# A two-layer trunk on one core: the order of the mixer's conv products, value products and scores, the place of the conv taps, and the splitting of the output weights

## The chip, the cores and the metric

The kernel runs on one NeuronCore of a Trainium2 chip. The core has five engines with an instruction queue each: PE (TensorE, matrix products), DVE (VectorE), ACT (ScalarE), POOL (GpSimd) and SP (SyncE, which here only starts transfers). POOL starts transfers too. An engine works through its queue in order; an instruction that waits for another engine, or for a transfer, holds up all that stands behind it on its own engine.

The metric is device time of one execution in microseconds (us), the median over several executions.

## The reference

The program computes a trunk of two layers on 512 tokens with 1024 features, in fp32. Each layer is a half-step feed-forward block, a mixer, another half-step feed-forward block and a norm. The change lies in the mixer alone:

```python
n = rms_norm(h, mix_norm[l]);  p = n @ w_in[l]
u_conv, q, k, v, q_mem = jnp.split(p, splits, axis=-1)
a, gate = jnp.split(u_conv, 2, axis=-1)              # 384 channels each
y = a * jax.nn.sigmoid(gate)
y = causal_depthwise_conv(y, w_dw, 31 taps) + b_dw
y_conv = jax.nn.silu(layer_norm(y, g, b))
y_swa = sliding_window_attention(rope(norm(q)), rope(norm(k)), v, sinks)  # 6 heads of 64, window 128
y_mem = memory_attention(norm(q_mem), mk, mv)                             # 4 heads, 256 memory rows
h = h + jnp.concatenate([y_conv, y_swa, y_mem], axis=-1) @ w_out[l]
h = h + 0.5 * swiglu(rms_norm(h, ffn2_norm[l]), ffn2_w1[l], ffn2_w3[l], ffn2_w2[l])
```

## The kernel before

**Layout.** Activations are held transposed: 128 partitions carry features of one of 8 chunks, 512 tokens lie along the free axis. Every product is made of three fp32r matmuls on a high and a low part of each operand (`mm3`, L172 to L176: hi·hi, then the two cross products). So each weight tile is loaded as a raw fp32 tile by SP (3 raw buffers, tag "raw") and split in two. `weights(..., V)` does it by an ACT copy (L143, the high part) and a DVE subtract (L144, the low part). `weights(..., G)` does it by two ACT copies (L148 the high part, L149 the negative of the raw tile) and a transfer that POOL starts and that adds the weights from memory to that negative (L150, about 0.9 us on POOL per start). The raw tile is free again when the last reader has read it: the DVE subtract in the first way, the second ACT copy in the other.

**Who sets the order.** A list of steps in the string `ORDER` is walked once per layer, and a scheduler that estimates durations decides how the work of these steps is interleaved on each engine; `tc.issue_after(x)` makes it place an instruction behind `x`. `queued()` places PE work behind the last matmul issued. The result is one fixed list per engine.

**The mixer's steps.** `c<c><i>`: half i of conv chunk c (24 matmuls of 128x512; half 1 holds the gate: a sigmoid on ACT, L669, then the gated input goes to `ypad`). `q`, `Q`: query products and their transposition to columns. `v`, `V`: value products (24 matmuls of 128x384) and their transposition. `a`: attention in ten groups of two (or one) 128-row blocks. For each group there are scores on PE, their row maxima on DVE (L751 and L752 for memory groups, L765 to L767 for window groups), Exp on ACT (L777), transposes on PE (L783) copied by ACT (L785), products with the values on PE (L794), division on DVE, and for a finished block transposes to the output operand (PE L817, ACT L143 `ghi`, DVE L144 `glo`). `t<c>`: the 31 taps of a conv chunk, one DVE instruction of 128x512 each (L871 the first, L874 the other 30), 93 per layer. `s`: the conv branch's layer norm and Silu: two sums over the three chunks on POOL (L880, L881), a matmul with ones that gives the mean (L883), three DVE subtracts of it (L886), squares on ACT (L234) added on DVE (L246), sums by matmul (L200), the root on POOL (L191), a spreading matmul (L213), the multiply (L891), Silu (L892) and a split.

**After the steps** stands the output product. For each of 8 output chunks there are 5 products with the attention's chunks (120 matmuls of 128x512 in all, weight tiles of 128x640, four split in each of the two ways) and then 3 with the conv chunks (72 matmuls, weight tiles of 128x768 named `ours`, one for two output chunks, split by ACT and DVE). The attention products need no result of the conv branch, so they are the work that PE has while the conv branch's norm is made. The next feed-forward block's weight tiles (128x1024, `in_w1b`, `in_w3b`) follow in the same raw buffers.

Of the kernel before, what the change touches and what calls it, by code (L numbers as in the profile page):

```python
# [18 lines left out]
P = 128  # L19
# [27 lines left out]
ORDER = "c00 c01 q0 c10 q1 c11 Q0 q2 v0 Q1 q3 v1 Q2 v2 v3 Q3 V0 V1 c20 V2 V3 a t0 t1 t2 s"  # L47
# [14 lines left out]
def trunk(ctx: ExitStack, tc: tile.TileContext, xT, memT, pos, w1a, w3a, w2a, w1b, w3b, w2b,  # L62
# [19 lines left out]
    def mm():  # L82

        turn[0] += 1
        return bank([P, S], "mm" if turn[0] % 4 else "cf")
# [526 lines left out]
    def mixer(l, x, st, last):  # L612
# [31 lines left out]

        def conv_half(c, i):
            nonlocal R
            ps = bank([P, S], "po") if c == 2 else mm()
            with queued():
                project(ps, weights(wconv[l, c, i], 1024, V if c + i < 2 else G, spare() if c == 2 else None), x)
            if c == 0:  # L650
                with queued():
                    if i == 0:
                        V.tensor_copy(rc, rms_cols(st, D))
                    else:
                        R = kept(spread(rc), "R", V)
            halves.append((c, i, ps))
            while halves and R is not None:
                gate(*halves.pop(0))
# [72 lines left out]
        def scored(kind, pairs):  # L731
# [17 lines left out]
            if not masked:  # L749
                for i in range(2):  # L750
                    V.tensor_reduce(out=nmr[:, b, i], in_=pp[i], axis=AX.X, op=ALU.max)  # L751
                V.scalar_tensor_tensor(out=nmr[:, b], in0=nmr[:, b], scalar=-1.0, in1=by_half(rm[:, b, :]), op0=ALU.mult, op1=ALU.mult)  # L752
                return pp, W
# [13 lines left out]
            V.tensor_tensor(out=at_(nmw), in0=at_(nmw), in1=per(nsinks), op=ALU.min)  # L767
# [3 lines left out]
        def turned(kind, b, c, scores, W):  # L771
# [3 lines left out]
            for i in range(2):  # L775
                n = 2 * c + i
                A.activation(pr[:, i, 0:W], scores[i], AF.Exp, bias=nm[:, b, i, c : c + 1], scale=rr[:, b, n : n + 1])  # L777
# [50 lines left out]

        def attention():
# [18 lines left out]
            s = scored(GROUPS[0][0], GROUPS[0][1:])  # L848
            conv_half(2, 1)
            yy.extend([gated_pair() for _ in range(KD // 2)][::-1])  # L850
            y.extend(at(p, ALL, i, ALL) for p in yy for i in range(2))
            for n, (kind, *pairs) in enumerate(GROUPS):
# [3 lines left out]
                if n + 1 < len(GROUPS):  # L856
                    nxt_s = scored(GROUPS[n + 1][0], GROUPS[n + 1][1:])
# [12 lines left out]
        def taps(c):  # L870
            V.tensor_scalar(out=cv[:, c, :], in0=ypad[:, c, 0:S], scalar1=conv_w[:, c, 0:1], scalar2=conv_b[:, c : c + 1],  # L871
                            op0=ALU.mult, op1=ALU.add)
            for j in range(1, TAPS):
                V.scalar_tensor_tensor(out=cv[:, c, :], in0=ypad[:, c, j : j + S], scalar=conv_w[:, c, j : j + 1],  # L874
                                       in1=cv[:, c, :], op0=ALU.mult, op1=ALU.add)
# [18 lines left out]

        for step in ORDER.split():
            f = {"c": conv_half, "q": queries, "Q": query_columns, "v": values, "V": value_columns, "a": attention, "t": taps,
                 "s": swish}[step[0]]
            f(*map(int, step[1:]))
# [3 lines left out]
        for d in range(KD):  # L902
            w = weights(wout[l, d, :, CCH:], 640, G if d < 4 else V)
# [9 lines left out]
        for i, own in enumerate(ours):  # L913
# [3 lines left out]
            split(own[0], own[1], raw[:, 0 : 2 * CCH], V)  # L917
# [132 lines left out]
```

## Time and profile before

| | |
|---|---|
| three runs | 1811.62, 1810.0, 1811.51 us; median 1811.51 us |
| profiled execution | 1811.26 us, of which its span on the core 1809.1 us |
| PE, DVE, ACT, POOL busy | 98%, 71%, 50%, 10% of the span |
| mean granted PE clock | 0.989 |
| moved by DMA | 250.44 MB, 138 GB/s on average |
| mixer of the first layer | from about 373 to 561 us of the span; its attention from about 455 to 510 |

Shares are of the span. A row of the timeline gives the start in us, the duration, the engine, the source line, the operation and its tiles; in square brackets stands how long the engine had been idle and what it waited for. The two layers run the same code, so rows of the first layer stand for both unless something else is said.

### The profile page before, as it was taken

To read this page: it belongs to the slowest core of one execution; us is meant where nothing else is said; L and a number is where in the kernel's file an instruction comes from. 1 tells how busy PE (TensorE), PEld (TensorE's weight loads), DVE (VectorE), ACT (ScalarE), POOL (GpSimd) and SP (SyncE) were. 2 spreads that over 40 slices of the span, in tenths; PEclk is the share of its full clock that TensorE was granted. 3 is DMA by queue.
4 is the path that set the end of the run, shared out by engine and by line. 5 is a ranking of instruction groups with operands and counts; after the bars stand their busy time and mean duration, and the time that the engine had idled before them with its cause. 6 is when DMAs were issued, how large, how long until landed. Compare 5 with 4: busy or idle time off the path is not lost.

```text
span 1809.1 us, 28077 instructions
## 1 busy us (share of the span) xinstructions
PE 1767.9 (98%) x10996; PEld 1585.8 (88%) x10996; DVE 1281.7 (71%) x1896; ACT 897.4 (50%) x1357; POOL 189.0 (10%) x207
## 2 busy tenths in 40 slices
PE   8999999999899999999999999999989999999997
PEld 6989999888688989898888898988877889898986
DVE  7969666569957857575678685766698567675755
ACT  5546444464655535353655463535456645453532
POOL 3001000025001000000010010000340010000000
PEclk9999999999899999999999999999999999999998
DMA  9466655275039456465556465643640666474622
GB/s 274 107 168 173 177 131 150 55 203 114 2 104 206 111 143 172 135 167 138 155 137 156 145 174 142 172 120 94 162 104 1 182 139 162 129 182 121 168 80 82
DMA packets 93589, 250.44 MB, mean 138 GB/s; under 512 B 9617, under 2 KB 11921, under 8 KB 93457
## 3 DMA queue, kind: packets, MB, share of 16 engines
q1 hardware_dynamic: 77040, 190.45, 34.9%
q0 software_dynamic: 16416, 58.20, 17.8%
q8 instruction: 86, 1.41, 0.3%
q14 instruction: 47, 0.38, 0.1%
HBM read 246.52 MB, written 2.10 MB: 137 GB/s over the span
## 4 chain that ended last, share of the span: by engine, by line
PE 79%; DVE 11%; issue 6%; ACT 2%; DMA 2%; SPq 0%; POOLq 0%; DVEq 0%; POOL 0%; ACTq 0%
PE mm L174 10%; PE mm L176 10%; PE mm L175 10%; PE po L176 9%; PE po L174 9%; PE po L175 9%; PE pt L174 6%; PE pt L175 6%; PE pt L176 6%; DVE there L874 6%; DMA raw<-in_wvm 1%; DVE wlo L144 1%; PE po L794 1%; DVE nmw L765 1%; ACT uu L777 0%
## 5 line engine op out<-in xcount | busy, mean ns | idle before, releaser
L143 ACT ACTIVATE whi<-raw 128x1024 fp32r<-128x1024 f32 (+3 forms) x360 | 337.9, 941 | 487.0 <-PE mm L175 235.7
L144 DVE TENSOR_TENSOR wlo<-raw,whi 128x1024 fp32r<-128x1024 f32 (+3 forms) x352 | 380.1, 1081 | 145.1 <-ACT whi L143 143.6
L175 PE MATMUL mm<-glo,whi 128*128 128x512 f32 x752 | 293.6, 391 | 0.0
L174 PE MATMUL mm<-ghi,whi 128*128 128x512 f32 x752 | 290.5, 391 | 0.7 <-ACT ghi L143 0.7
L176 PE MATMUL mm<-ghi,wlo 128*128 128x512 f32 x734 | 285.6, 389 | 0.0
L176 PE MATMUL po<-mh,wlo 128*128 128x256 f32 x864 | 244.6, 283 | 1.1 <-DVE wlo L144 1.1
L174 PE MATMUL po<-mh,whi 128*128 128x256 f32 x864 | 244.7, 283 | 0.2 <-ACT part L386 0.2
L175 PE MATMUL po<-ml,whi 128*128 128x256 f32 x864 | 244.5, 283 | 0.0
L176 PE MATMUL pt<-xhi,wlo 128*128 128x256 f32 x864 | 244.0, 283 | 0.0
L175 PE MATMUL pt<-xlo,whi 128*128 128x256 f32 x864 | 243.9, 283 | 0.0
L174 PE MATMUL pt<-xhi,whi 128*128 128x256 f32 x864 | 243.0, 283 | 0.3 <-ACT xhi L143 0.3
L464 DVE SCALAR_TENSOR_TENSOR h<-mm,h 128x512 f32<-128x512 f32 x128 | 87.7, 688 | 138.1 <-PE mm L176 138.1
L174 PEld LDWEIGHTS mm<-ghi,whi 128*128 128x128 f32 x752 | 141.2, 188 | 30.3 <-ACT ghi L143 1.2
L176 PEld LDWEIGHTS po<-mh,wlo 128*128 128x128 f32 x864 | 165.8, 192 | 1.3 <-DVE wlo L144 1.3
L174 PEld LDWEIGHTS po<-mh,whi 128*128 128x128 f32 x864 | 165.8, 192 | 1.2 <-ACT part L386 0.4
L175 PEld LDWEIGHTS pt<-xlo,whi 128*128 128x128 f32 x864 | 165.7, 192 | 0.8
L175 PEld LDWEIGHTS po<-ml,whi 128*128 128x128 f32 x864 | 165.8, 192 | 0.6
L174 PEld LDWEIGHTS pt<-xhi,whi 128*128 128x128 f32 x864 | 165.1, 192 | 1.4 <-ACT xhi L143 0.5
L175 PEld LDWEIGHTS mm<-glo,whi 128*128 128x128 f32 x752 | 141.3, 188 | 28.3 <-issue 0.5
L176 PEld LDWEIGHTS pt<-xhi,wlo 128*128 128x128 f32 x864 | 165.6, 192 | 0.0
L176 PEld LDWEIGHTS mm<-ghi,wlo 128*128 128x128 f32 x734 | 137.8, 188 | 29.0 <-issue 0.5
L874 DVE SCALAR_TENSOR_TENSOR there<-ypad,par,there 128x512 f32<-128x512 f32 x180 | 135.5, 764 | 1.4
(314 smaller groups left out, 3305.9 us busy)
## 6 DMA issues: line engine op xcount, KB each, us to landing
raw<-in_w2a SPq DMA_DIRECT2D x48, 384.0 KB, 3.6
raw<-in_w2b SPq DMA_DIRECT2D x48, 384.0 KB, 3.5
raw<-in_w1b SPq DMA_DIRECT2D x26, 512.0 KB, 3.7
raw<-in_w3b SPq DMA_DIRECT2D x26, 512.0 KB, 3.7
raw<-in_w1a SPq DMA_DIRECT2D x25, 512.0 KB, 3.7
raw<-in_w3a SPq DMA_DIRECT2D x25, 512.0 KB, 3.7
wsum<-in_w1a SPq DMA_DIRECT2D x18, 512.0 KB, 4.4
wsum<-in_w3a SPq DMA_DIRECT2D x18, 512.0 KB, 4.3
```

The source lines that it names most:

```text
L143: A.activation(hi, x, AF.Copy)
L144: on.tensor_tensor(out=lo, in0=x, in1=hi.bitcast(F32), op=ALU.subtract)
L174: T.matmul(ps, a[0], b[0], start=first, stop=False, **more)
L175: T.matmul(ps, a[0], b[1], start=False, stop=False, **more)
L176: tail[0] = T.matmul(ps, a[1], b[0], start=False, stop=last, **more)
L464: added = V.scalar_tensor_tensor(out=h[:, d, :], in0=ps, scalar=0.5, in1=h[:, d, :], op0=ALU.mult, op1=ALU.add)
L765: V.tensor_reduce(out=each(nmw, i), in_=pp[i], axis=AX.X, op=ALU.max)
L794: tail[0] = T.matmul(po[:, 2 * c + i, :], ptb[:, i, j, :], v, start=(j == 0), stop=(j == nk - 1))
L874: V.scalar_tensor_tensor(out=cv[:, c, :], in0=ypad[:, c, j : j + S], scalar=conv_w[:, c, j : j + 1], in1=cv[:, c, :], op0=ALU.mult, op1=AL ...
```

## The change

Five edits, all in the mixer, each made in both layers:

1. The third conv chunk's two halves (`c20`, `c21`) come before the value products. The second of them was issued inside attention, behind the first group's scores. Both now use the general PSUM banks and the general weight buffers.
2. The value weights are split half by DVE and half by POOL transfers, into spare tiles, and the last two value products use other banks. The first two groups' scores (`g0`, `g1`) are issued between the value products.
3. Of the 93 taps of a layer the first 48 are free. Tap number 48+n is placed behind the maxima of group n//2, at most group 9, so 27 taps stand behind the last group's maxima.
4. The eight attention-part tiles of the output weights are split only after an Exp of the sixth group.
5. The conv-part tiles (`ours`) are split by two ACT copies and two POOL transfers each in place of an ACT copy and a DVE subtract.

```diff
-ORDER = "c00 c01 q0 c10 q1 c11 Q0 q2 v0 Q1 q3 v1 Q2 v2 v3 Q3 V0 V1 c20 V2 V3 a t0 t1 t2 s"
+EARLY = 48
+ORDER = "c00 c01 q0 c10 q1 c11 Q0 q2 q3 Q1 c20 c21 Q2 v0 Q3 v1 V0 V1 g0 v2 V2 g1 v3 V3 a t0 t1 t2 s"
...
         def conv_half(c, i):
             nonlocal R
-            ps = bank([P, S], "po") if c == 2 else mm()
+            ps = mm()
             with queued():
-                project(ps, weights(wconv[l, c, i], 1024, V if c + i < 2 else G, spare() if c == 2 else None), x)
+                project(ps, weights(wconv[l, c, i], 1024, V if c + i < 2 else G), x)
...
         def values(t):
             if not t:
-                ww["v"] = [weights(wvm[l, i], 768, V) for i in range(4)]
-            ps = mm()
+                ww["v"] = [weights(wvm[l, i], 768, V if i < 2 else G, spare()) for i in range(4)]
+            ps = mm() if t < 2 else bank([P, S], "po")
...
             V.scalar_tensor_tensor(out=at_(nmw), in0=at_(nmw), scalar=-1.0, in1=rr, op0=ALU.mult, op1=ALU.mult)
-            V.tensor_tensor(out=at_(nmw), in0=at_(nmw), in1=per(nsinks), op=ALU.min)
+            biased[len(biased)] = V.tensor_tensor(out=at_(nmw), in0=at_(nmw), in1=per(nsinks), op=ALU.min)
...
-                A.activation(pr[:, i, 0:W], scores[i], AF.Exp, bias=nm[:, b, i, c : c + 1], scale=rr[:, b, n : n + 1])
+                raised[kind, b] = A.activation(pr[:, i, 0:W], scores[i], AF.Exp, bias=nm[:, b, i, c : c + 1], scale=rr[:, b, n : n + 1])
...
+        begun = {}
+
+        def begin(n):
+            begun[n] = scored(GROUPS[n][0], GROUPS[n][1:])
...
-            s = scored(GROUPS[0][0], GROUPS[0][1:])
-            conv_half(2, 1)
+            s = begun[0]
...
                 if n + 1 < len(GROUPS):
-                    nxt_s = scored(GROUPS[n + 1][0], GROUPS[n + 1][1:])
+                    if n + 1 not in begun:
+                        begin(n + 1)
+                    nxt_s = begun[n + 1]
...
             for j in range(1, TAPS):
-                V.scalar_tensor_tensor(out=cv[:, c, :], in0=ypad[:, c, j : j + S], scalar=conv_w[:, c, j : j + 1],
-                                       in1=cv[:, c, :], op0=ALU.mult, op1=ALU.add)
+
+                n = c * TAPS + j - EARLY
+                with tc.issue_after(biased[min(n // 2, len(GROUPS) - 1)].ins) if n >= 0 else nullcontext():
+                    V.scalar_tensor_tensor(out=cv[:, c, :], in0=ypad[:, c, j : j + S], scalar=conv_w[:, c, j : j + 1],
+                                           in1=cv[:, c, :], op0=ALU.mult, op1=ALU.add)
...
         for d in range(KD):
-            w = weights(wout[l, d, :, CCH:], 640, G if d < 4 else V)
+            with tc.issue_after(raised["w", 2].ins):
+                w = weights(wout[l, d, :, CCH:], 640, G if d < 4 else V)
...
-            split(own[0], own[1], raw[:, 0 : 2 * CCH], V)
+            A.activation(own[0], raw[:, 0 : 2 * CCH], AF.Copy)
+            A.activation(own[1], raw[:, 0 : 2 * CCH], AF.Copy, scale=-1.0)
+            for j in range(2):
+                G.dma_start(own[1][:, blk(j, CCH)], wout[l, 2 * i + j, :, 0:CCH], accum_op=ALU.add)
```

The engines' lists show what this moves. The changed kernel has its own line numbers: L888 a tap, L894 and L895 POOL's two sums, L897 the mean's matmul, L201 the norm's sums, L900 the subtracts of the mean, L932, L933 and L935 the copies and transfers of the `ours` tiles; other lines are 1 higher than before up to the scores and 4 or 5 higher in attention.

POOL's list around the conv branch's sums in the first layer, before (`esw` are sinks of window groups, `wlo<-in_wout` the transfers of edit 4's tiles):

```order
L150 DMA wlo<-in_wout 128x640
L543 TENSOR_TENSOR rm<-hv_4274,nhalf 128x4
L150 DMA wlo<-in_wout 128x640
L880 TENSOR_TENSOR aux_3744<-there 128x512
L768 TENSOR_TENSOR esw<-nmw,rw 128x6
L768 TENSOR_TENSOR esw<-nmw,rw 128x2x2 x2
L768 TENSOR_TENSOR esw<-nmw,rw 128x4
L768 TENSOR_TENSOR esw<-nmw,rw 128x2x2
L768 TENSOR_TENSOR esw<-nmw,rw 128x2
L881 TENSOR_TENSOR aux_3744<-aux_3744,there 128x512
L191 TENSOR_TENSOR rsq_4929<-ms_4927,nhalf 128x4
```

and of the change:

```order
L773 TENSOR_TENSOR esw<-nmw,rw 128x4
L151 DMA wlo<-in_wout 128x640 x2
L894 TENSOR_TENSOR aux_3744<-there 128x512
L151 DMA wlo<-in_wout 128x640 x2
L773 TENSOR_TENSOR esw<-nmw,rw 128x2x2
L773 TENSOR_TENSOR esw<-nmw,rw 128x2
L935 DMA whi<-in_wout 128x384 x6
L895 TENSOR_TENSOR aux_3744<-aux_3744,there 128x512
L935 DMA whi<-in_wout 128x384 x2
L192 TENSOR_TENSOR rsq_4931<-ms_4929,nhalf 128x4
```

Six of the eight new transfers stand ahead of the second sum (four in the second layer), and the output weights' transfers have moved from before the first sum into attention.

PE's list in the first layer from attention's last transposes (L817) to the mean (L883), before; the sums L200 follow 32 more products later, the spreading matmul L213 25 products after them:

```order
L817 MATMUL pt<-cst,aux_3743 128x128 x2
L175 MATMUL mm<-glo,whi 128x512
L176 MATMUL mm<-ghi,wlo 128x512
L175 MATMUL mm<-glo,whi 128x512
L176 MATMUL mm<-ghi,wlo 128x512
L175 MATMUL mm<-glo,whi 128x512
L176 MATMUL mm<-ghi,wlo 128x512
L174 MATMUL mm<-ghi,whi 128x512 x3
L883 MATMUL pt<-aux_3744,onesq 128x512
```

and in the change, where 72 products stand between the last transposes (L822) and the mean (L897) in both layers, of which the last three are shown:

```order
L175 MATMUL po<-ghi,whi 128x512
L176 MATMUL po<-glo,whi 128x512
L177 MATMUL po<-ghi,wlo 128x512
L897 MATMUL pt<-aux_3744,onesq 128x512
L201 MATMUL cf<-onesq,st 128x1 x4
L201 MATMUL cf<-onesq,sq 128x1 x4
L175 MATMUL cf<-ghi,whi 128x512
L176 MATMUL cf<-glo,whi 128x512
```

The sums now follow the mean with nothing between; 15 products stand between them and the spreading matmul.

DVE's list of the change in the first layer, from attention's last low part (`glo`) to the subtracts of the mean (`wlo` are low parts of output weights, and of 128x1024 of the next feed-forward block's):

```order
L145 TENSOR_TENSOR glo<-pt,ghi 128x2x128
L888 SCALAR_TENSOR_TENSOR there<-ypad,par,there 128x512 x8
L145 TENSOR_TENSOR wlo<-raw,whi 128x640
L888 SCALAR_TENSOR_TENSOR there<-ypad,par,there 128x512
L145 TENSOR_TENSOR wlo<-raw,whi 128x640
L888 SCALAR_TENSOR_TENSOR there<-ypad,par,there 128x512
L145 TENSOR_TENSOR wlo<-raw,whi 128x640
L888 SCALAR_TENSOR_TENSOR there<-ypad,par,there 128x512 x4
L145 TENSOR_TENSOR wlo<-raw,whi 128x640
L888 SCALAR_TENSOR_TENSOR there<-ypad,par,there 128x512 x4
L145 TENSOR_TENSOR wlo<-raw,whi 128x1024
L900 SCALAR_TENSOR_TENSOR there<-pt,there 128x512 x3
```

In the list before, the last tap stands ahead of the last group's maxima, so none of these taps is there.

More of the change, by code (lines that the diff above doesn't have):

```diff
@@ L643, in spare @@
             return tuple(z.rearrange("p i s -> p (i s)") for z in gated_pair())
+        biased, raised = {}, {}
         def conv_half(c, i):
             nonlocal R
-            ps = bank([P, S], "po") if c == 2 else mm()
+            ps = mm()
             with queued():
-                project(ps, weights(wconv[l, c, i], 1024, V if c + i < 2 else G, spare() if c == 2 else None), x)
+                project(ps, weights(wconv[l, c, i], 1024, V if c + i < 2 else G), x)
             if c == 0:
@@ L751, in scored @@
                     V.tensor_reduce(out=nmr[:, b, i], in_=pp[i], axis=AX.X, op=ALU.max)
-                V.scalar_tensor_tensor(out=nmr[:, b], in0=nmr[:, b], scalar=-1.0, in1=by_half(rm[:, b, :]), op0=ALU.mult, op1=ALU.mult)
+                biased[len(biased)] = V.scalar_tensor_tensor(out=nmr[:, b], in0=nmr[:, b], scalar=-1.0, in1=by_half(rm[:, b, :]),
+                                                             op0=ALU.mult, op1=ALU.mult)
                 return pp, W
@@ L895, in mixer @@
         for step in ORDER.split():
-            f = {"c": conv_half, "q": queries, "Q": query_columns, "v": values, "V": value_columns, "a": attention, "t": taps,
-                 "s": swish}[step[0]]
+            f = {"c": conv_half, "q": queries, "Q": query_columns, "v": values, "V": value_columns, "g": begin, "a": attention,
+                 "t": taps, "s": swish}[step[0]]
             f(*map(int, step[1:]))
```

## The prediction

> **What bounds the kernel now.** I read the page's busy shares first, then its chain of waits, then the mixer in windows. Line numbers are the kernel's before; the changed kernel's own numbers stand where I say so.
>
> ```profile
> PE 1767.9 (98%) x10996; PEld 1585.8 (88%) x10996; DVE 1281.7 (71%) x1896; ACT 897.4 (50%) x1357; POOL 189.0 (10%) x207
> ...
> PE 79%; DVE 11%; issue 6%; ACT 2%; DMA 2%; SPq 0%; POOLq 0%; DVEq 0%; POOL 0%; ACTq 0%
> ```
>
> PE is busy for 1767.9 of 1809.1 us, so all stalls together are 41 us. An edit that leaves PE's products alone can win what of this lies in the mixer, twice (two layers); it can lose any amount. The windows of layer 0 show where the mixer loses it (columns: us, then busy time of PE, PEld, DVE, ACT, POOL, then PE's granted clock, DMA share, GB/s):
>
> ```profile
> core 0: us, PE busy (x) PEld busy (x) DVE busy (x) ACT busy (x) POOL busy (x), PEclk, DMA share, GB/s
> ...
> 440.00:450.00 10.00, 8.61 (x44) 6.71 (x45) 9.79 (x18) 4.33 (x12) 7.78 (x7) 1.00 0.91 194
> 450.00:460.00 10.00, 8.10 (x39) 5.36 (x37) 9.82 (x17) 4.23 (x6) 1.19 (x1) 0.95 0.24 45
> 460.00:470.00 10.00, 8.55 (x47) 7.89 (x47) 7.21 (x16) 6.35 (x12) 0.26 (x2) 0.53 0.00 0
> 470.00:500.00 30.00, 27.76 (x216) 22.00 (x215) 28.43 (x68) 21.62 (x52) 2.98 (x7) 1.00 0.01 1
> 500.00:510.00 10.00, 8.69 (x63) 7.51 (x62) 5.06 (x14) 5.32 (x12) 0.63 (x1) 1.00 0.01 2
> 510.00:520.00 10.00, 10.00 (x50) 8.10 (x49) 4.23 (x6) 4.05 (x6) 0.00 (x0) 1.00 0.17 36
> ...
> 1353.00:1363.00 10.00, 8.01 (x52) 6.84 (x50) 7.52 (x17) 6.96 (x11) 0.74 (x1) 0.66 0.01 2
> ```
>
> Attention runs from 455 to 510. DVE is full before and during it (9.8 of 10, 28.43 of 30); PE idles 8.3 us between 440 and 510 and has half its clock (0.53) in 460 to 470. From 510 on PE has no gap, while DVE is idle more than half the time: this tail is where work could be put, and it now hides the conv branch's norm.
>
> **Part A, the start of attention.** The third conv chunk's second half leaves attention, and two groups' scores go between value products.
>
> ```profile
> 441.93 0.44 PE L570 MATMUL pt<-cst,aux 128*128 128x128 f32 x2 [1.39 <-ACT here L701]
> 455.74 1.28 ACT L777 ACT_TABLE_LOAD   x1 [6.98 <-DVE nmr L752]
> 457.04 1.93 ACT L777 ACTIVATE uu<-mm,nmr,rm 128x256 f32<-128x256 f32 x4
> 457.66 2.03 PE L783 MATMUL pt<-cst,uu 128*128 128x128 f32 x8 [1.54 <-ACT uu L777]
> 458.99 1.28 ACT L669 ACT_TABLE_LOAD   x1
> 460.28 0.63 ACT L669 ACTIVATE aux<-aux 128x512 f32<-128x512 f32 x1
> 461.45 1.75 PE L794 MATMUL po<-mvn,aux 128*128 128x65 f32 x7 [1.77 <-ACT aux L785]
> ```
>
> Three stalls (1.39, 1.54, 1.77) make 4.7 us. The second comes from maxima that stand among taps on a full DVE, the third from the sigmoid (L669) and its table load in front of the copy that PE wants. Ten us at a clock of 0.53 cost at most another 4.7. So the gain is at most 9.4. Against it: V1, V2 and V3 now follow their own products directly, and each can pay the 1.39 of a product's copy (4.2), and the Exp load with four Exps (3.2) can stand ahead of a value copy: 7.4, which leaves +2.7 if the clock stays low. Between −9.4 and +2.7 I take **−4**, near the middle and somewhat to the gain, since the sigmoid certainly leaves.
>
> The sigmoid's removal saves two table loads per layer (Exp, sigmoid, Exp becomes Exp). The rows price them at 1.28 each. [...]
>
> **Part B, inside attention.** Taps that stood between the maxima go behind them, and eight ACT copies of output weights (four pairs L148, L149) now wait for an Exp of the sixth group, so they land in attention; six stand in one run ahead of a copy that PE needs.
>
> ```profile
> 436.46 0.75 ACT L149 ACTIVATE wlo<-raw 128x640 fp32r<-128x640 f32 x1
> 437.09 0.75 ACT L148 ACTIVATE whi<-raw 128x640 fp32r<-128x640 f32 x1
> ```
>
> They are 0.63 apart: six take 3.9, eight 5.0, which is the upper end. The lower end is −3.5: all of PE's idle time in 470 to 510 (2.24 and 1.31) goes. The run of six stands in one in-order queue before `ghi` and `aux` copies that the next transposes need, so most is paid: **+3**.
>
> **Part C, the conv branch's mean.** In before every tap is done before the last group's maxima:
>
> ```profile
> 498.49 0.73 DVE L874 SCALAR_TENSOR_TENSOR there<-ypad,par,there 128x512 f32<-128x512 f32 x1
> 499.37 1.27 POOL L881 TENSOR_TENSOR aux<-aux,there 128x512 f32<-128x512 f32 x1 [0.86 <-DVE there L874]
> 501.13 0.68 DVE L751 TENSOR_REDUCE nmr<-cf 128x2 f32<-128x512 f32 x1
> ```
>
> Now 27 taps are queued behind those maxima, and 18 behind attention's last `glo`, mixed with the four subtracts of output weights in this order: 8 taps, subtract, tap, subtract, tap, subtract, 4 taps, subtract, 4 taps (two in layer 1, whose other two come earlier). Before the mean's second POOL sum stand six POOL transfers (four in layer 1), each pair waiting for two ACT copies of a weight tile, whose raw buffer is freed by one of those subtracts. All prices:
>
> ```profile
> 508.23 0.38 PE L817 MATMUL pt<-cst,aux 128*128 128x128 f32 x2
> 509.06 0.42 DVE L144 TENSOR_TENSOR glo<-pt,ghi 128x256 fp32r<-128x256 f32 x1 [0.49 <-ACT ghi L143]
> 509.14 0.39 PE L176 MATMUL mm<-ghi,wlo 128*128 128x512 f32 x1
> 509.37 0.39 PE L175 MATMUL mm<-glo,whi 128*128 128x512 f32 x1
> ...
> 446.32 5.48 DVE L874 SCALAR_TENSOR_TENSOR there<-ypad,par,there 128x512 f32<-128x512 f32 x7
> 516.24 0.82 DVE L144 TENSOR_TENSOR wlo<-raw,whi 128x640 fp32r<-128x640 f32 x1 [1.99 <-ACT whi L143]
> 522.29 0.85 ACT L143 ACTIVATE whi<-raw 128x768 fp32r<-128x768 f32 x1 [2.69 <-DMA raw<-in_wout]
> 532.93 1.05 ACT L143 ACTIVATE whi<-raw 128x1024 fp32r<-128x1024 f32 x1
> 444.59 0.90 POOL L150 DMA_DIRECT2D wlo<-in_wout  x1
> ...
> raw<-in_w1b SPq DMA_DIRECT2D x4, 512.0 KB, 5.0
> raw<-in_wout SPq DMA_DIRECT2D x8, 192.0 KB, 2.9
> ```
>
> Count from PE's last transposes (508.61 in before). PE then has 72 products at 0.23: 16.5. DVE starts 0.9 later (509.48). A tap is (5.48−0.75)/6 = 0.79. The fourth subtract ends at 0.9 + 14×0.79 + 4×0.82 = 15.2, the taps at 18.4. The third weight tile's raw load begins at 15.2, lands at 18.1, ACT's two copies end at 19.8, POOL's two issues at 21.6, and the sum (1.27) at **22.9**; without transfers ahead of it, 19.7.
>
> A second path meets it: DVE's subtract of the next feed-forward tile (128x1024) stands ahead of the three subtracts of the mean. Its load follows the weight tiles on SP, starting about 16.6 when ACT has finished the second; landed at 21.6, copied by ACT (1.05) at 22.7, subtracted by about 23.8 (1.1, estimated from 0.82 for 640 columns and 1.08 as its group's mean). So the mean's subtracts start near 24 in both layers.
>
> ```profile
> L144 DVE TENSOR_TENSOR wlo<-raw,whi 128x1024 fp32r<-128x1024 f32 (+3 forms) x352 | 380.1, 1081 | 145.1 <-ACT whi L143 143.6 <-PE mm L176 0.5
> ...
> 510.51 1.02 PE L883 MATMUL pt<-aux,onesq 128*128 128x512 f32 x2
> 511.57 1.89 DVE L886 SCALAR_TENSOR_TENSOR there<-pt,there 128x512 f32<-128x512 f32 x3 [2.08 <-PE pt L883]
> 513.56 0.69 DVE L246 TENSOR_TENSOR st<-st,sq 128x512 f32<-128x512 f32 x1
> ...
> 518.67 0.95 PE L200 MATMUL cf<-onesq,st 128*128 128x1 f32 x8
> 526.18 1.05 PE L213 MATMUL pt<-cst,rsq 128*128 128x128 f32 x8
> ```
>
> From subtracts to the squares' last add is 514.25−511.57 = 2.7. In before, products filled PE from the mean (510.51) to the sums (518.67); in the change the sums stand directly behind the mean, so PE waits until 24 + 2.7 = 26.7. Its own work ends at 17.2 (products and 0.7 for the mean): 9.5, and six handovers at 0.1 to 0.5 (0.49 at `glo`) add 1.5: **+11** where the mean and the sums wait together. Ends: 6 if the taps alone decide (19.7 + 1.0 for the mean + 2.7 − 17.2), 13 if loads or ACT lag by two us more.
>
> **Part D, the rest.** Between spread and conv products 27 to 30 products (6.2 to 6.9 us) cover the norm's multiply and Silu, which in before took from 526.18 to about ACT's row at 532.93, 6.8: 0 to 1.5, I take **+1**. The four DVE subtracts that go (conv weights) lie in a tail where DVE has room: nothing, unless the taps fill it, which is counted. **Clock**: after stalls of 1.5 to 1.8 us among short work the windows show ten us at 0.53 and 0.66, a loss of 3.4 to 4.7; a wait of ten us before full products can bring the same: **+3**, ends 0 and 5.
>
> [...]
>
> **Sum.** −4 + 3 + 11 + 1 + 3 = +14 per layer; layer 1 repeats the same mixer, so +28. The profiled execution took 1811.26 us (span 1809.1 and 2.2 around it), the median of the runs is 1811.51: 1811.3 + 28 = **1839**.
>
> **Rivals.** *Only the taps are late* (weight tiles arrive early, POOL is free): C is 6, clock 2: −4+3+6+1+2 = 8, twice 16: 1827. For it: POOL is busy 10% of the span and idle after 500; against: three raw buffers, each freed by a subtract among taps. *The other side*: attention gives everything, A −9.4 and B −3.5, because DVE no longer delays maxima and the clock stays up; then with C at 6 and nothing else −6.9, twice −14: 1797. It decides if A and B together pass −C. For it: DVE is full to 470; against: PE's idle rows there name ACT, which gets more work. *The change moves nothing*, since gains and the tail cancel (A+B about −10, C about 10): 1811. *Everything bad*: A +2.7, B +5, C 13, D 1.5, clock 5 = 27: 1865.
>
> **Chances.** Forecast (1830 to 1855) 0.63, only taps late (1816 to 1830) 0.16, worse (above 1855) 0.07, no net change 0.05, other side 0.09. 0.2%, about 3.6 us, is what a measurement of this kernel can tell from no change: faster 0.09, same 0.05, slower 0.86. The likeliest case's own range is 1830 to 1855; 8 times in 10 the time should lie between 1817 and 1858.
>
> **What would show it.** In the changed profile: a PE idle of 3 to 9 us at the mean (its L897) named after POOL's second sum, and one of 3 to 8 at the sums (its L201) named after DVE, 10 to 13 together; taps (its L888) still running 18 us after the last transposes; only one Exp table load in the mixer's start and no slow clock there; a PE stall near 4 us in mid-attention behind ACT's weight copies. If PE enters the mean within 4 us of its products' end in both layers and the sums follow without a second wait, the forecast is wrong by 10 us or more; if attention itself is over 8 us shorter, the sign may be.

## The result, and the profile after

The changed kernel takes 1872.56 us (median of four runs, 1869.19 to 1875.55) where the kernel before takes 1810.76 (four runs beside it, 1809.39 to 1811.62): a ratio of 1.0342 with a 95% interval of 1.0319 to 1.0364. It is slower by 62 us; 28 were forecast, and the time lies above the range. The profiled execution, the slowest of the four at 1875.55 us, has a span of 1873.8 us, 64.7 more than before.

The page of the changed kernel, busy shares and the chain of waits:

```profile
PE 1794.3 (96%) x10996; PEld 1604.7 (86%) x10996; DVE 1276.4 (68%) x1884; ACT 899.8 (48%) x1365; POOL 205.8 (11%) x227
...
PE 74%; DVE 11%; issue 6%; DMA 4%; ACT 4%; SPq 0%; POOLq 0%; DVEq 0%; POOL 0%; ACTq 0%
```

PE's matmuls are the same 10996, but they took 26 us longer (1794.3 against 1767.9): that is, for the most part, lost clock (24.6 us by the sums below). The other 38 us are idle time of PE (79.5 us against 41.2). Both lie in the two mixers, as the windows by stage show. For each layer the first row runs from attention's start to its last transposes, the second from there to the spreading matmul of the conv branch's norm. Before:

```profile
455.00:508.23 53.23, 46.33 (x328) 37.42 (x328) 44.82 (x103) 37.13 (x79) 5.06 (x8) 0.90 0.00 1
508.23:526.18 17.95, 17.95 (x87) 14.78 (x86) 8.17 (x13) 6.87 (x10) 1.03 (x1) 1.00 0.28 76
...
1348.70:1400.74 52.04, 44.80 (x329) 35.95 (x329) 44.72 (x103) 37.06 (x79) 5.07 (x8) 0.93 0.00 1
1400.74:1418.69 17.95, 17.95 (x87) 14.78 (x86) 7.77 (x12) 6.46 (x10) 1.03 (x1) 1.00 0.28 75
```

and after (the first row starts a few us earlier in the work, since scores begin before the last value products):

```profile
452.00:514.14 62.14, 52.52 (x356) 43.62 (x356) 38.46 (x92) 39.47 (x91) 10.60 (x13) 0.89 0.20 43
514.14:556.00 41.86, 29.68 (x109) 23.31 (x108) 21.10 (x30) 12.35 (x18) 9.36 (x10) 0.72 0.53 134
...
1376.00:1441.60 65.60, 57.02 (x355) 47.67 (x356) 39.24 (x92) 39.32 (x90) 10.62 (x13) 0.80 0.19 41
1441.60:1481.84 40.24, 27.79 (x109) 21.89 (x108) 20.18 (x30) 12.37 (x19) 9.37 (x10) 0.78 0.55 139
```

In the tail PE went from no gap at full clock to 12 us of idle time at a clock of 0.72 and 0.78. The waits themselves, PE's rows with an idle time over 2 us in the first layer and the tail's two of the second:

```profile
454.39 0.44 PE L571 MATMUL pt<-cst,aux 128*128 128x128 f32 x2 [3.27 <-ACT aux L717]
...
488.95 0.66 PE L788 MATMUL pt<-cst,uu 128*128 128x128 f32 x4 [3.63 <-ACT aux L790]
...
541.43 2.07 PE L897 MATMUL pt<-aux,onesq 128*128 128x512 f32 x2 [9.00 <-POOL aux L895]
546.43 1.87 PE L201 MATMUL cf<-onesq,st 128*128 128x1 f32 x8 [2.92 <-DVE st L247]
588.30 1.15 PE L201 MATMUL cf<-onesq,st 128*128 128x1 f32 x8 [2.16 <-DVE st L247]
...
1464.03 2.07 PE L897 MATMUL pt<-aux,onesq 128*128 128x512 f32 x2 [5.27 <-POOL aux L895]
1473.03 1.86 PE L201 MATMUL cf<-onesq,st 128*128 128x1 f32 x8 [6.92 <-DVE st L247]
```

The mean and the sums wait 11.9 us together in the first layer and 12.2 in the second. And this is what the clock does behind such waits, three stretches of the changed kernel in windows:

```profile
1414.00:1424.00 10.00, 10.00 (x44) 8.53 (x45) 4.45 (x12) 6.72 (x14) 2.73 (x4) 0.50 0.98 216
507.50:517.00 9.50, 9.13 (x34) 7.85 (x34) 7.12 (x15) 1.64 (x4) 0.00 (x0) 0.50 0.01 2
534.00:554.00 20.00, 9.39 (x27) 6.96 (x28) 5.01 (x8) 6.04 (x8) 7.91 (x9) 0.51 0.88 213
```

Behind a single wait in mid-attention PE works for ten us without a gap at half its clock (first row).

For all kernels below I cut the two mixers (360 to 620 us and 1240 to 1540 us of the span) into windows of 2 us and added up PE's idle time, and its busy time times (1 − granted clock), the lost clock. Before: 18.6 idle and 10.4 lost. After: 57.1 and 35.0. The growth, 38.5 + 24.6 = 63.1 us, is the 64.7 of the span but for 1.6. The two sums come from one profile per kernel, the ratios from all its runs.

### The profile page after: what moved, and what is told of

It is laid out like the page before. It is cut to its first block, busy times and chain, and to the rows that moved or that the text cites. A ratio compares the mean times of both kernels' runs of the same rounds, so it can differ in the third digit from the quotient of the medians.

```text
span 1873.8 us, 28084 instructions
## 1 busy us (share of the span) xinstructions
PE 1794.3 (96%) x10996; PEld 1604.7 (86%) x10996; DVE 1276.4 (68%) x1884; ACT 899.8 (48%) x1365; POOL 205.8 (11%) x227
## 4 chain that ended last, share of the span: by engine, by line
PE 74%; DVE 11%; issue 6%; DMA 4%; ACT 4%; SPq 0%; POOLq 0%; DVEq 0%; POOL 0%; ACTq 0%
PE mm L175 10%; PE mm L176 10%; PE mm L177 10%; PE po L175 8%; PE po L176 8%; PE po L177 8%; PE pt L175 5%; PE pt L176 5%; PE pt L177 5%; DVE there L888 4%; DMA raw<-in_wconv 1%; PE po L799 1%; DVE wlo L145 1%; DVE xlo L155 1%; DMA raw<-in_w1b 1%
## 5 line engine op out<-in xcount | busy, mean ns | idle before, releaser
L144 ACT ACTIVATE whi<-raw 128x1024 fp32r<-128x1024 f32 (+3 forms) x344 | 324.5, 946 | 486.0 <-PE mm L176 245.6
L145 DVE TENSOR_TENSOR wlo<-raw,whi 128x1024 fp32r<-128x1024 f32 (+3 forms) x344 | 373.0, 1085 | 147.5 <-ACT whi L144 133.7
L888 DVE SCALAR_TENSOR_TENSOR there<-ypad,par,there 128x512 f32<-128x512 f32 x180 | 135.5, 761 | 2.2
```

Of the source, the lines that this page charges most:

```text
L144: A.activation(hi, x, AF.Copy)
L145: on.tensor_tensor(out=lo, in0=x, in1=hi.bitcast(F32), op=ALU.subtract)
```

## The experiments

Ratios are to the kernel before, with 95% intervals; idle and lost clock are the two sums just described. Runs with the whole change less one part come first, then single parts on the kernel before, then runs that test a cause. In e8 and e9 PE's waits are filled with matmuls that nobody reads; these count as busy, which lowers the idle time.

| run | ratio | idle | lost clock |
|---|---|---|---|
| the change | 1.0342 [1.0319, 1.0364] | 57.1 | 35.0 |
| less edit 5 (e1) | 1.0293 [1.0248, 1.0338] | 56.0 | 29.6 |
| less edit 3 (e2) | 1.0136 [1.0114, 1.0157] | 38.4 | 17.3 |
| less edit 4 (e3) | 1.0201 [1.0179, 1.0224] | 48.3 | 19.8 |
| edits 1 and 2 alone (e4) | 1.0066 [1.0046, 1.0086] | 29.6 | 14.4 |
| edit 3 alone (e5) | 1.0165 [1.0135, 1.0195] | 40.1 | 15.8 |
| edits 1, 2, taps spread (e6) | 1.0028 [1.0011, 1.0045] | 23.5 | 13.1 |
| products first (e7) | 1.0287 [1.026, 1.0315] | 54.5 | 28.5 |
| e7, waits filled (e8) | 1.0296 [1.0275, 1.0317] | 36.2 | 23.8 |
| e7, filled longer (e9) | 1.0243 [1.021, 1.0275] | 32.2 | 16.6 |
| edit 4 alone (e10) | 1.0037 [1.002, 1.0054] | 25.5 | 15.9 |
| edit 5 alone (e11) | 1.0006 [0.9984, 1.0027] | 20.6 | 11.6 |
| e1, tiles behind taps (e12) | 1.0295 [1.0269, 1.0321] | 53.0 | 23.3 |
| before, taps spread (e13) | 0.9994 [0.9982, 1.0007] | 18.9 | 11.7 |
| another order, taps spread (e14) | 0.9997 [0.9981, 1.0013] | 20.7 | 9.8 |

### e1: the conv-part tiles split by DVE again

```diff
-            A.activation(own[0], raw[:, 0 : 2 * CCH], AF.Copy)
-            A.activation(own[1], raw[:, 0 : 2 * CCH], AF.Copy, scale=-1.0)
-            for j in range(2):
-                G.dma_start(own[1][:, blk(j, CCH)], wout[l, 2 * i + j, :, 0:CCH], accum_op=ALU.add)
+            split(own[0], own[1], raw[:, 0 : 2 * CCH], V)
```

> The change with its fifth edit undone: the conv-part weight tiles are split by ACT and a DVE subtract again, so no POOL transfer stands ahead of the second POOL sum. In the changed kernel that sum starts 4.2 us after the last tap has ended (535.16 to 539.43). Theory POOL (the prediction's path): the wait at the mean and at the sums falls from 11.9 and 12.2 us to about 7 per layer and the time from 1872.6 to about 1860. Rival TAPS: the taps behind the maxima and the weight subtracts among them are enough; the waits together stay at 10 to 13 us per layer and the time within 4 us of 1872.6.

1865.96 us, between the two expectations; its interval overlaps that of the change. PE's waits in this run's first layer, and DVE and POOL just before them:

```profile
525.78 0.96 DVE L145 TENSOR_TENSOR whi<-raw,whi 128x768 fp32r<-128x768 f32 x1 [1.05 <-ACT whi L144]
...
533.89 0.75 DVE L888 SCALAR_TENSOR_TENSOR there<-ypad,par,there 128x512 f32<-128x512 f32 x1
...
534.79 1.26 POOL L895 TENSOR_TENSOR aux<-aux,there 128x512 f32<-128x512 f32 x1 [34.56 <-DVE there L888]
...
536.10 2.07 PE L897 MATMUL pt<-aux,onesq 128*128 128x512 f32 x2 [8.77 <-POOL aux L895]
540.95 1.87 PE L201 MATMUL cf<-onesq,st 128*128 128x1 f32 x8 [2.77 <-DVE st L247]
```

POOL has nothing ahead of its sum, idles for 34.56 us, and starts it when the last tap ends (534.64). The waits are 8.77 + 2.77 = 11.5 us, as in the change. So POOL's transfers, which the prediction named, are not needed for them. The tiles' subtracts now stand among the taps on DVE, each waiting for its raw tile, and hold the taps back: the last tap ends 23.7 us after the last transposes where it ended 20.4 after them in the change, which takes back most of the 4.3 us that POOL's transfers had stood between that tap and the sum.

### e2: all taps free

```diff
-EARLY = 48
+EARLY = 93
```

> The change with its third edit undone: all 93 taps are free again. Theory TAPS: no wait at the mean, the sums or the next block's first sums (11.9 + 0.3 + 2.2 us in the first layer, 12.2 + 2.2 in the second) and a clock of 1.00 from the last transposes to the next block (in the changed kernel it is 0.50 for 20 us there): 14 + 5 us per layer, about 1834. Rival (the taps were also in the way of attention): the waits in attention grow by 3 to 6 us per layer, since DVE is full there again, and the time stays at 1842 to 1850. If POOL's transfers alone were the cause, the wait at the mean would stay above 5 us and the time above 1860.

1838.42 us, 37 less by the ratios. The tail is whole again, in this run's windows:

```profile
519.00:573.00 54.00, 53.93 (x251) 44.02 (x250) 27.73 (x43) 33.67 (x48) 12.41 (x14) 1.00 0.77 202
```

No wait and a clock of 1.00 from 519 to 573, the transfers of edit 5 still in place. Attention pays, in PE's row at the value columns:

```profile
456.50 0.69 PE L571 MATMUL pt<-cst,aux 128*128 128x128 f32 x2 [7.51 <-ACT aux L717]
```

It waits 7.51 us there where the change had 3.27: both sentences of the expectation hold, and the time lies between them.

### e3: output weights free to be split before attention

```diff
-            with tc.issue_after(raised["w", 2].ins):
-                w = weights(wout[l, d, :, CCH:], 640, G if d < 4 else V)
+            w = weights(wout[l, d, :, CCH:], 640, G if d < 4 else V)
```

> The change with its fourth edit undone: the output weights may be split before attention. Theory BURST: the wait of 3.63 us at the transposes in mid-attention goes, and with it the clock of 0.50 behind it (3 us in the first layer, 13 in the second): 3.6 plus 1.7 and 5.7, twice in all about 13 us, so 1860. Rival: the copies then delay value or query columns before attention by the same amount, and the time stays within 4 us of 1872.6.

1850.88 us, 26 less than the change by the ratios, twice what was expected. The 3.63 us wait is gone in both layers. Lost clock fell by 15.2 us and idle time by 8.8: the edit was dear for the clock. In the change 7.5 us of clock are lost behind that wait, from 490.13 and 1411.73 on. Another 8.1 are lost from 507.20 and 1435.63 on, behind waits of 1.49 and 0.97 us for an Exp at attention's end (PE L788), which are 0.84 in e3 and have no slow clock behind them. In the change the ACT rows ahead of the long wait are the run of six copies:

```profile
484.37 0.75 ACT L149 ACTIVATE whi<-raw 128x640 fp32r<-128x640 f32 x1
...
487.50 0.74 ACT L150 ACTIVATE wlo<-raw 128x640 fp32r<-128x640 f32 x1
488.13 0.28 ACT L144 ACTIVATE ghi<-pt 128x128 fp32r<-128x128 f32 x1
488.28 0.61 ACT L790 ACTIVATE aux<-pt 128x512 f32<-128x512 f32 x1
```

### e4: only the new order and the value weights

Edits 3, 4 and 5 undone as above.

> Only the first two edits are left (the order of conv, value products and first scores, and the splitting of value weights); taps free, output weights unbound, conv-part tiles split by ACT and DVE. The prediction's part A says a gain of 4 us per layer: about 1803. Rival: value columns wait for ACT copies that stand behind maxima or Exps (0.8 and 3.3 us in the changed kernel) and more so with free taps on DVE, with a slow clock behind each: a loss of 5 to 12 us per layer, 1821 to 1835.

1825.78 us, 12 slower than before: the gain of part A does not exist. PE's waits of this run:

```profile
PE pt L571 <- ACT aux L717: 13.6, 6, 6.0
...
PE mm L176 <- DMA glo<-in_wvm: 4.8, 2, 2.9
```

The value columns wait 13.6 us in all for the copies of value products (L717), up to 6.0 at a time. Two value products wait 4.8 for the weights that POOL's transfers now complete. Why the copies are late can be read in the change itself, on ACT:

```profile
450.49 1.28 ACT L782 ACT_TABLE_LOAD   x1 [4.66 <-DVE nmr L756]
451.79 1.93 ACT L782 ACTIVATE uu<-mm,nmr,rm 128x256 f32<-128x256 f32 x4
453.60 0.38 ACT L715 ACTIVATE here<-po,rc 128x128 f32<-128x128 f32 x1
453.84 0.49 ACT L717 ACTIVATE aux<-po,rc 128x256 f32<-128x256 f32 x1
```

The first group's Exps stand ahead of the value copy in ACT's queue and wait for that group's maxima (L756), which stand among taps on DVE. The prediction had the table load and the Exps (3.2 us) ahead of a copy, but not ACT's wait for the maxima in front of them.

### e5: the queued taps alone

The third edit on the kernel before, nothing else:

```diff
+                n = c * TAPS + j - EARLY
+                with tc.issue_after(biased[min(n // 2, len(GROUPS) - 1)].ins) if n >= 0 else nullcontext():
+                    V.scalar_tensor_tensor(out=cv[:, c, :], ...)
```

> The kernel before with the third edit alone (45 of 93 taps queued behind the groups' maxima, 27 of them behind the last). The own-by-DVE run kept its waits of 11.5 and 10.9 us without any of the new POOL transfers. Theory TAPS: here too PE waits 10 to 13 us per layer at the mean and the sums and 2.2 at the next block's sums, with the clock at 0.50 behind them, which is 5 us more per layer; some of PE's waits at attention's start go (1.5 to 4 us per layer): 1838 to 1852. Rival: the waits need the late weight copies or the transfers as well: under 1826.

1841.87 us. PE's waits of this run:

```profile
PE pt L888 <- POOL aux L886: 19.8, 2, 10.1
PE cf L201 <- DVE st L247: 10.8, 5, 2.8
```

The whole of the tail's loss is here with no other edit: 10.07 + 2.77 us in the first layer, 9.75 + 2.77 in the second, and 2.16 at the next block's sums.

### e6: the taps queued, but none behind the last maxima

On e4, 45 taps queued five to a group, at most behind the ninth group of ten:

```diff
-                with tc.issue_after(biased[min(n // 2, len(GROUPS) - 1)].ins) if n >= 0 else nullcontext():
+                with tc.issue_after(biased[min(n // 5, 8)].ins) if n >= 0 else nullcontext():
```

> The order-alone kernel with 45 taps queued behind maxima again, but five to a group and none behind the last group's. Theory: the 12 us in the tail come from the 27 taps behind the last maxima alone, and a free DVE at attention's start is worth something: no wait at the mean, the value columns' wait of 4.8 and 6.0 us shrinks to about 3.3: 1815 to 1823 beside 1826 for the order alone. Rival: any queueing of taps delays the mean: above 1835.

1817.65 us, 7 less than e4 by the ratios. No wait in the tail, and the value columns' long wait falls from 4.8 and 6.0 us to 1.21 in both layers. So queueing as such does the tail no harm, and taking taps from ahead of the first maxima helps the copies. What costs is the 27 taps behind the last maxima.

### e7, e8, e9: the price of the clock

Output chunks 4 and 5 are issued ahead of chunk 3 (e7); then matmuls that nobody reads fill the waits, n ahead of the mean and m ahead of the sums (e8: 26 and 18, e9: 30 and 28). DVE, POOL and ACT do the same work in all three.

```diff
+            last = tail[0]
+            for i in range(n):
+                with tc.issue_after(last.ins):
+                    last = T.matmul(pm, x[0][:, 0, 0:P], x[0][:, 1, :], start=True, stop=True)
+            with tc.issue_after(last.ins):
+                mean = T.matmul(pm, onesq, s1, start=True, stop=True)
```

> A control for the next run: the change with output chunks 4 and 5 issued ahead of chunk 3, so that all 75 products that can precede the mean stand ahead of it in the program's text too. Same waits as the change (11 to 13 us per layer in the tail): 1866 to 1876.

> The control with 26 matmuls of 128x512 that nobody reads put on PE ahead of the mean and 18 ahead of the norm's sums, so that PE is busy in most of the tail's waits while DVE, POOL and ACT work as before. Theory CLOCK: the products behind the waits run at half speed only because PE idled; with PE busy the clock stays at 1.00 there and 4 to 6 us per layer go: 8 to 12 us under the control. Rival: the chain through DVE sets the end whatever PE's clock is, or the clock falls without idling: within 3 us of the control.

> The control of before with 30 matmuls ahead of the mean and 28 ahead of the sums (26 and 18 left waits of 0.7 and 1.7 us, and the clock still fell to 0.50 for 7 us behind the second one). The fillers now take 13.2 us per layer where the control waited 11.9 and 10.0, so they cost 1 to 3 us per layer themselves. Theory CLOCK: no wait is left, the clock stays at 1.00 between mean and spread, and the sums and 15 products behind them take about 4.5 us in place of 9: net 1 to 4 us per layer under the control's 1864, 1856 to 1862. Rival: the clock falls there whether or not PE waits, and the time is 1866 to 1872.

1864.15, 1866.74 and 1858.27 us. e7 came out a little under its expected range. The windows from the sums to the spreading matmul, the same sums and 15 products on PE (the first of the columns is the stretch, the third from the end the granted clock). In e7:

```profile
540.95:549.91 8.96, 8.71 (x31) 7.60 (x32) 0.16 (x1) 0.00 (x0) 1.03 (x1) 0.60 0.35 93
```

In e8:

```profile
542.01:550.74 8.73, 8.47 (x31) 7.05 (x32) 0.16 (x1) 0.00 (x0) 1.03 (x1) 0.61 0.43 108
```

And in e9:

```profile
542.24:547.97 5.73, 5.47 (x33) 4.78 (x33) 0.16 (x1) 0.00 (x0) 1.03 (x1) 1.00 0.54 144
```

e8 missed its expectation: with only 0.7 us of waiting left at the mean and 1.7 at the sums, the clock fell all the same, and nothing was gained. With no wait left (e9) it stayed at 1.00 and the same work took 3.0 to 3.2 us less. The ratios of e9 and e7 differ by 8 us, but their intervals still touch. From the last transposes to the spreading matmul, where the fillers act, e9 needs 3.2 us less than e7 in the first layer and 2.3 in the second, where the fillers run on past the end of the wait and the sums start 1.8 us later. What the windows settle is that the half clock there follows PE's waiting and is not set by the other engines.

### e10, e11: edits 4 and 5 alone on the kernel before

> The kernel before with the fourth edit alone. In the change this edit's undoing was worth 22 us. Theory BURST: a wait of 3 to 4.5 us in mid-attention behind the run of ACT copies, with half a clock behind it, and later weight tiles: 6 to 10 us per layer, 1823 to 1832. Rival: the 22 us were for the most part its effect on the late taps, and alone it costs under 3 us per layer: under 1817.

1821.32 us, a ratio of 1.0037 or 7 us, between the two expectations. The wait behind the copies is there in both layers, in PE's row of the first:

```profile
490.28 1.12 PE L785 MATMUL pt<-cst,uu 128*128 128x128 f32 x4 [4.33 <-ACT aux L787]
```

It takes the place of shorter waits, and the lost clock grows by only 5.5 us. In the whole change its undoing was worth 26 us. The slow clock behind the wait itself is no dearer there: it costs 8.5 us in e10 and 7.5 in the change, and lasts 13.7 us in the second layer of both. What e10 does not have is the slow clock at attention's end, 8.1 us (e3). It does not always stand there: the profiles of e9 and e12, with the same edits in attention, have none at that place. The rest of the 26 us I have not separated.

> The kernel before with the fifth edit alone: eight DVE subtracts fewer, eight ACT copies and 16 POOL transfers more in the whole program, in a tail where DVE and POOL have room. Expected: no wait at the mean, since all taps are done before; at most one wait near 1.4 us at the conv products behind the Silu's split: within 4 us of before, 1809 to 1815. Rival: POOL's transfers stand ahead of the norm's root (L191 before) and PE waits for it at the spread: 3 us per layer or more, above 1817.

1816.32 us, a ratio of 1.0006: no difference. Edit 5 costs nothing that can be measured by itself. In the company of the late taps the ratios of the change and of e1 differ by 9 us, but their intervals overlap, so that it costs something there is not shown.

### e12: are the late tiles or the late taps the cause?

e1 with the tiles' splitting queued behind the last tap:

```diff
-            split(own[0], own[1], raw[:, 0 : 2 * CCH], V)
+            with tc.issue_after(biased["tap"].ins):
+                split(own[0], own[1], raw[:, 0 : 2 * CCH], V)
```

> The own-by-DVE kernel with the conv-part tiles' splitting queued behind the last tap, so that no tap waits for those tiles (in that run they held taps for 3 to 5 us and the waits were 8.8 at the mean and 2.8 at the sums). Theory PACE (the norm's chain is late as a whole: taps and weight tiles share DVE and the raw buffers, whichever stands first): the wait at the mean falls to 4 or 5 us, the one at the sums grows to 6 or 8, their sum stays at 10 to 13, and the time stays within 5 us of that run, 1861 to 1871. Rival: the tiles alone held the mean; both waits together fall under 7 us and the time to 1850 to 1858.

1868.58 us, a ratio of 1.0295 where e1 had 1.0293. The profile is of the fastest of its four runs, at 1858.08. PE's two waits in the first layer:

```profile
530.48 2.07 PE L897 MATMUL pt<-aux,onesq 128*128 128x512 f32 x2 [4.80 <-POOL aux L895]
537.93 1.87 PE L201 MATMUL cf<-onesq,st 128*128 128x1 f32 x8 [5.38 <-DVE st L247]
```

4.80 + 5.38 = 10.2 where e1 had 11.5. Counted from the last transposes the taps are done 4.5 us earlier, and the wait moves from the mean to the sums, behind the tiles' subtracts. The chain is late as a whole; which of its users of DVE goes first decides only where PE waits.

### e13, e14: is there a faster version?

e13 is the kernel before with 33 taps queued, `biased[min(n // 4, 8)]` from tap 61 on. e14 is e6 with the order `c00 c01 q0 c10 q1 Q0 q2 q3 c11 Q1 c20 Q2 v0 Q3 v1 c21 V0 v2 g0 V1 V2 v3 V3` and `biased[min(n // 5, 6)]`.

> The kernel before with its own order and 33 taps (from the 61st on) queued four to a group behind the groups' maxima, none behind the last group's. Theory: queueing that keeps every tap ahead of the last maxima leaves the tail free and only takes taps out of the maxima's way in mid-attention: 0 to 4 us faster, ratio 0.998 to 1.000. Rival: any tap that is held costs, ratio over 1.002.

> The change's first two edits in another order (c00 c01 q0 c10 q1 Q0 q2 q3 c11 Q1 c20 Q2 v0 Q3 v1 c21 V0 v2 g0 V1 V2 v3 V3, one group's scores begun early), 45 taps queued five to a group and none behind the seventh, the fourth and fifth edits left out. Theory: with no sigmoid between Exps and no tap ahead of the first maxima, the value column's wait of 1.2 to 6 us of the order-alone and taps-spread kernels falls to about 1, and attention's start keeps its clock: 2 to 6 us faster than before, ratio 0.997 to 0.999. Rival: waits at other places take it back, ratio 1.000 to 1.004 as for taps spread.

1813.35 and 1813.46 us beside 1813.79 for the kernel before: both are the same as before within their intervals. In e14 the value columns still wait 2.3 us, more than expected. No version here beats the kernel before.

## Why the prediction was wrong

The direction was right, and so were the place and the size of the largest term, the size in part by luck. Two steps failed, the clock above all, and the time fell outside the range. The table holds each part's forecast per layer against what the two layers lost more than before, from the profiles. A runs from the mixer's first product to 470 us before and after (1364 and 1394 in the second layer), B from there to the last transposes, C to the spreading matmul, D the 54 us behind it.

| part | forecast | idle time, layer 1 and 2 | lost clock, layer 1 and 2 |
|---|---|---|---|
| A | −4 | +2.3, +2.2 | −4.2, −1.0 |
| B | +3 | +2.5, +1.7 | +5.3, +8.9 |
| C | +11 | +12.2, +12.4 | +6.5, +4.5 |
| D | +1 | +2.3, +2.4 | +1.7, +3.4 |
| clock | +3, in C | | |

**Part A** took −4 per layer, and this step failed: it counted 4.7 us of waits as gone, and PE waits 2.3 us longer than before. With the clock that came back that makes −1.9 and +1.1. But 1.7 us of this clock in each layer are a stretch at the mixer's very start in the profile of before (from 380.59 and 1274.88 on), ahead of all that the edits move; without it A is −0.2 and +2.8, at its upper end of +2.7. With part B it made −1 in the forecast; from the mixer's first product to attention's last transposes the change took 5.2 us more in the first layer and 10.3 in the second (129.9 to 135.1, 128.7 to 139.0). The sigmoid left as foreseen, but the scores that were moved ahead put the Exps in front of the value copies, a wait of 3.3 us. The prediction had priced that, at 3.2, and weighed it too little. Where more taps stand ahead of the maxima the wait grows to 4.8 and 6.0 (e4), since the Exps wait for the maxima first; that was in no bound. And 1.1 us went to value weights that wait for a POOL transfer, which was not in the list at all. The four table loads that went, 1.28 us each, show as no gain where ACT waits 4.66 us for maxima ahead of the load that is left (450.49); that load ends at 451.77 and the Exps start at 451.79.

**Part B**, the run of six copies, was right as a wait: 3.6 us where 3.9 us of copies were named, and +3 was taken. The clock lost behind it and at attention's end, 5.3 and 8.9 us, was in no term.

**Part C** was right in size, 11.9 and 12.2 us for 11, and in its sum of two waits with the second path through the feed-forward tile. Its reason was half right. POOL's transfers ahead of the second sum do stand in the way in the change (rows below), but e1 shows that they are not needed, and the rival "only the taps are late", priced at 6, was priced too low: whoever splits the tiles, the taps or the norm wait for them. What I missed is the first subtract. ACT's copy for it waited for PE to free the pair of weight buffers, and DVE waited behind it with ten taps still to do:

```profile
523.18 0.74 ACT L144 ACTIVATE whi<-raw 128x640 fp32r<-128x640 f32 x1 [7.99 <-PE mm L176]
...
523.95 0.82 DVE L145 TENSOR_TENSOR wlo<-raw,whi 128x640 fp32r<-128x640 f32 x1 [2.13 <-ACT whi L144]
532.05 3.11 DVE L888 SCALAR_TENSOR_TENSOR there<-ypad,par,there 128x512 f32<-128x512 f32 x4
...
538.34 1.75 POOL L935 DMA_DIRECT2D whi<-in_wout  x2 [2.25 <-ACT whi L933]
539.43 1.95 POOL L895 TENSOR_TENSOR aux<-aux,there 128x512 f32<-128x512 f32 x1
```

The chain ended 3.5 us later than worked out: the sums start at 546.43, 31.7 after the last transposes' end at 514.77, for 28.2 with the handovers. PE's own work took 2.5 us longer than the 17.2 worked out, with the granted clock at 0.50 from 507.20 to 517.44 and again under the mean. The two errors nearly cancel, so that the wait fitted is luck.

**Part D** took 1; the next block's sums wait 2.2, in both layers, and e2 and e4, without late taps, have no such wait. It is not the wait that was named: behind the Silu PE waits under 0.2 us.

**The clock** took 3 per layer with an upper end of 5, and this is the step that failed most: 24.6 us more are lost over two layers, 12 per layer. I took one stretch of ten us at half clock per layer as the worst case, from the rows of before, and only behind the tail's wait. But the waits in mid-attention and at the next block's sums bring theirs as well: in the change's first layer the clock is at 0.50 from 456, 490, 507, 534 and 589 on, and in the second from 1378, 1412, 1435, 1463 and 1514 on. These stretches last from 3.41 us (456.00 to 459.41) to 20.48 (534.51 to 554.99): the longest is twice the ten that I took as the worst.

In sum, per layer: A and B −1 forecast, 4.4 measured as idle time; C and D 12 forecast, 14.7 measured; clock 3 forecast, 12 measured. The case "everything bad", at 1865, came nearest; its 5 us of clock per layer was the bound that was far too low. The edits one by one cost 12 (e4), 30 (e5), 7 (e10) and 1 us (e11), 50 together where the change costs 62. Their idle time adds up (41.4 us against 38.5 of the change); it is the lost clock that does not (16.1 against 24.6).

## What to carry to other kernels

When work is taken out of the way of one stage, count what the next stage hides behind: here the conv norm was free because it was done while PE had products without a dependence on it, and queueing the taps, 27 of them past that point, cost 30 us alone (e5). Price each new wait of PE twice, once for the idle time and once for the half clock that can follow it (here 38.5 us of idle time more and 24.6 of lost clock), and count that per wait and not per stage. And when an instruction is moved ahead in an engine's in-order queue, price what it waits for, not only what it does: here the first Exps took 3.2 us with their table load, and ACT waited 4.66 for the maxima in front of them.

## What was not expected of the hardware

- Behind a wait of 1.7 us and matmuls of one column the granted clock was halved for nearly 7 us (e8: 0.52 from 543.7 to 550.5), while the kernel before waits 0.93 us at its 502.70 and keeps 1.00. The length of the wait alone does not decide: the change waits 0.97 us up to 1433.02 and runs at 0.50 from 1435.63 on.
- The granted clock that the profiles record changes in steps of 3.41 us. In windows of the profiles of before, of the change and of e9 to e14 the stretches of half clock in the mixers last one to six such steps, and in each profile their starts lie whole numbers of steps apart, as on the lines of one grid with cells of that length: in the change's first layer they start at 456.00, 490.13, 507.20, 534.51 and 589.12 (10, 5, 8 and 16 steps apart) and last 1, 1, 3, 6 and 1 steps. Two waits of nearly one length fell differently on the grid and ended differently. The value columns' wait of 3.32 us in e12 (449.27 to 452.59) is shared by two cells, in which PE is busy for 1.62 and 1.88 us, and the clock stays at 1.00 (first two rows below). In e7 the same wait, 3.47 us (448.79 to 452.25), falls almost whole into one cell, and the next cell is at half clock (last two rows). That this made the difference is not shown: in the change PE is busy for 2.20 us of the cell from 1432.22 to 1435.63, more than in either cell of e12, and half clock follows all the same.

```profile
447.65:451.06 3.41, 1.62 (x10) 1.30 (x8) 2.27 (x5) 2.36 (x4) 0.59 (x1) 1.00 0.00 0
451.06:454.47 3.41, 1.88 (x12) 1.34 (x13) 0.93 (x3) 2.23 (x6) 0.83 (x1) 1.00 0.00 0
...
449.21:452.62 3.41, 0.36 (x2) 0.20 (x2) 0.53 (x2) 3.35 (x8) 0.00 (x0) 1.00 0.00 0
452.62:456.03 3.41, 3.41 (x13) 2.59 (x13) 1.86 (x4) 0.38 (x1) 1.01 (x1) 0.50 0.00 0
```

- The half clock can last far beyond the wait that starts it: 10.00 us of 10 busy at 0.50 behind a 3.63 us wait in the second layer, four steps of the grid in all, and one step, 3.4 us, behind the same wait in the first. No run here tells why it stays for four.
- PE idle time and lost clock add up to the time: over the kernels without fillers their growth against before meets the growth of the span within 4 us, most of them within 2.
